# Gating, transposes and sums of h in steps of one K block, and a fourth branch's chunks moved between two passes, in a hybrid decoder layer on one core

## The chip, the cores and the metric

The kernel runs on one core of one Trainium2 chip. A core has a matrix engine (TensorE; PE in the rows, PEld for its weight loads), a vector engine (VectorE, DVE), a scalar engine (ScalarE, ACT), a general engine (GpSimd, POOL) and a sync engine (SyncE, SP) that here only issues DMAs. Each engine works through its own queue in the order in which the program was written. The metric is the device time of one execution in microseconds (us), lower is better; the median of three runs is compared.

## The reference

One layer, 512 tokens, width 2048, everything in float32. Four mixers run side by side on one normalised input; their outputs are normalised per branch and go through one output projection; then a SwiGLU FFN of width 5632 and a last normalisation.

```python
h = rmsnorm(x, norm_mix_g[l])
proj = h @ w_in[l]
pa, pb, pc, pd = jnp.split(proj, IN_SPLITS, axis=-1)
ya = merge_heads(mixer_dilated(*split_qkv_heads(pa), bias_a))    # branch A
yb = mixer_sgu(pb, ...)                                          # branch B
yc = merge_heads(mixer_moba(*split_qkv_heads(pc), bias_c))       # branch C
yd = mixer_rwkv7(pd, ...)                                        # branch D
ycat = rmsnorm(jnp.stack([ya, yb, yc, yd], axis=2), branch_norm_g[l]...)
x = x + ycat.reshape(B, S, D_MIX) @ w_out[l]
h = rmsnorm(x, norm_ffn_g[l])
x = x + (jax.nn.silu(h @ w_gate[l]) * (h @ w_up[l])) @ w_down[l]
return rmsnorm(x, norm_final_g)
```

## The kernel before

Each matrix product is made of three matmuls on operands that are split into a high and a low part: high by high, high by low, low by high. `split2` (L1041) makes the parts: ScalarE copies the source into the high part (L1043), VectorE subtracts it from the source for the low part (L1044). A weight chunk or block is loaded by SyncE, split by ScalarE and VectorE, and then used by TensorE in the program's order; `run` (L933) calls every generator in the list `side` once after each half block of matmuls. So the order of all work around the matmuls is set by where a generator yields.

**Output projection.** 32 chunks of 512 rows by 256 columns, in the order of the list `chunks`. The first pass has 8 column groups g of three chunks (branches D, B, C, numbered 3, 1, 2); `add_x2` adds its sums to the residual `x2`. Beside it the generator `attention(0, 0)` computes branch A, in 45 steps. The second pass has 8 chunks, branch A alone, one per g, and feeds the FFN: `on_last` (L1278) calls `make_x2` (add, gain, store of x), `split_a11`, `first_sums` of the group before, and the squares. `gemm` (L132) takes chunks from `next_chunk`, which issues the split of the chunk after it; the split's two tiles are taken from four (`wsp`), so they are free again when the matmuls of a chunk are done. After this pass `late_sums` runs in `side`: the last `first_sums`, eight sums of the second kind, eight splits.

**FFN up.** The products with `w_gate` and `w_up` are a Strassen-like scheme of seven products P1 to P7 on halves of tokens (th 0 and 1), of K and of gate and up. The 5632 columns are 11 groups `gi`; in each the seven products come in the order P1, P5, P6, P3, P7, P4, P2, each as four blocks (`strassen(k)`) of two K tiles, 12 matmuls of 128x128 by 512 columns to a block. `w_ahead(k)` sums the weights of block k+3 (`w_sum`: T for P5, P6, P4, in place for P7) and splits those of block k+2 (`w_split`, high part in one of 3 tiles, low in one of 4), and lets SyncE load up to block k+8, with at most 12 raw tiles of the 79 of the pool `p2`, which hold nearly all else too. `got_product` takes the results: c11 is kept after P1, c22 after P5, c12 after P6; P3 and P7 are added to c12 and c22. After P4, and after P2's add to c11, `gated` applies Silu (ScalarE, L1223) and the multiply (VectorE, L1224) to each of the two token tiles, one after the other, and appends `turn_h`, which waits four half blocks, then transposes 2 x 8 tiles on TensorE and calls `h_sums` (L1182) each time: the sums and splits that the down projection's own seven products need, each stored to DRAM (`ad`) by a DMA that ScalarE issues.

**FFN down.** `ds` lists 7 x 22 products (p, kk) in an order: P1 with P5, P6 with P3, then P7 and P4 with P2 strewn in after every second one. `d_ahead(i)` loads up to item i+4 and splits up to i+2 (T, high part `dh`, low part `dl`). Items 0 and 1 are begun under the last FFN blocks (`begin_down`); then `finish_all` runs out the `side` list, the pools `sums` (with `fp`) and `mid` (with `p2`) are closed, and the pool `dn` is opened on their memory. The last three items are done tile by tile at the end (`tail`), and after each of four token tiles `finish_tok` takes the mean square, scales and stores.

## Time and profile before

| what | value |
|---|---|
| runs before | 2351.2, 2355.08, 2352.35 us; median 2352.35 |
| the profiled execution | 2354.43 us, its span 2352.7 us, mean granted clock 0.985 |
| TensorE, PEld busy in the span | 2245.9 us (95%), 1793.7 us (76%) |
| VectorE, ScalarE busy | 1567.0 us (67%), 1013.7 us (43%) |
| high part 128x512, 128x1024 on ScalarE | 0.62, 1.06 us |
| low part 128x512, 128x1024 on VectorE | 0.69, 1.22 us |
| last store issued, end of span | 2348.68, 2352.7 us |

Times in the rows count from the start of the span. A matmul's record overlaps with the next one's, so stops of TensorE are best seen from start to start. A row of a timeline ends, in brackets, with the idle time before it on its engine and what ended that. A store or load is issued in a fraction of a microsecond and lands later. The two clock levels of TensorE are 1.2 and 2.4 GHz; the granted clock in the rows is the mean share of the higher one.

### The profile page before, as it was taken

What the parts mean: (1) busy time and instruction counts of PE and PEld (TensorE: products, weight loads), DVE (VectorE), ACT (ScalarE), POOL (GpSimd) and SP (SyncE); (2) the same over time, 40 slices, a digit from 0 to 9 for tenths busy, and PEclk for the clock granted to TensorE, in tenths of its full rate; (3) what the DMA queues carried; (4) which work ended last, traced back from release to release, by engine and by line L of the source; (5) the groups of instructions that cost most, each with busy time, mean ns of one, the idle gap of its engine ahead of it and who ended that gap; (6) DMA issues with size and microseconds to landing.
All of it is one profiled execution on the core that took longest, in us unless ns stands there. A gap on an engine that the chain in (4) does not pass through costs nothing.

```text
span 2352.7 us, 29300 instructions
## 1 busy us (share of the span) xinstructions
PE 2245.9 (95%) x11064; PEld 1793.7 (76%) x11064; DVE 1567.0 (67%) x2341; ACT 1013.7 (43%) x1556; POOL 2.3 (0%) x16
## 2 busy tenths in 40 slices
PE   8999999999999997899999999999999879999996
PEld 6788878877777785678777777877877768888785
DVE  6555456654444447877867877777787667777775
ACT  5522222244444435544444444444445344543334
POOL 0000000000000000000000000000000000000000
PEclk9999999999999999999999999999999989999998
DMA  5232323232233235343444455354355187547884
GB/s 185 84 95 73 101 76 92 61 99 82 71 99 108 90 109 178 118 164 121 166 161 152 149 169 180 114 189 166 117 170 192 52 289 250 175 130 241 284 299 177
DMA packets 164541, 342.78 MB, mean 146 GB/s; under 512 B 29296, under 2 KB 34928, under 8 KB 164400
## 3 DMA queue, kind: packets, MB, share of 16 engines
q1 hardware_dynamic: 134832, 290.25, 38.6%
q10 hardware_dynamic: 29568, 50.66, 6.0%
q8 instruction: 87, 1.43, 0.3%
q14 instruction: 54, 0.44, 0.1%
HBM read 302.79 MB, written 38.05 MB: 145 GB/s over the span
## 4 chain that ended last, share of the span: by engine, by line
PE 73%; DVE 13%; ACT 7%; issue 4%; DMA 1%; ACTq 1%; SPq 0%; DVEq 0%
PE prod L1266 8%; PE prod L1267 8%; PE prod L1265 8%; PE acc L144 7%; PE acc L146 7%; PE acc L145 7%; PE bk L1340 4%; PE bk L1341 4%; PE bk L1339 4%; DVE wl L1044 3%; PE acc L162 3%; PE acc L164 2%; PE acc L163 2%; ACT wh L1043 2%; DVE dl L1044 2%
## 5 line engine op out<-in xcount | busy, mean ns | idle before, releaser
L1044 DVE TENSOR_TENSOR wl<-wq,wh 128x512 fp32r<-128x512 f32 x352 | 227.2, 687 | 116.2 <-ACT wh L1043 115.2
L1266 PE MATMUL prod<-wl,h 128*128 128x512 f32 x704 | 282.1, 401 | 22.3 <-DVE wl L1044 22.2
L1265 PE MATMUL prod<-wh,h 128*128 128x512 f32 x704 | 281.5, 400 | 16.4 <-ACT wh L1043 16.4
L1267 PE MATMUL prod<-wh,l 128*128 128x512 f32 x704 | 279.3, 397 | 0.0
L1043 ACT ACTIVATE wh<-wq 128x512 fp32r<-128x512 f32 x352 | 201.4, 623 | 176.0 <-PE prod L1267 105.5
L1339 PE MATMUL bk<-dh,ah 128*128 128x512 f32 x608 | 238.7, 393 | 19.2 <-ACT dh L1043 19.2
L106 DVE TENSOR_TENSOR wlo<-wraw,whi 128x1024 fp32r<-128x1024 f32 x127 | 155.3, 1223 | 140.1 <-ACT whi L105 139.8
L1340 PE MATMUL bk<-dl,ah 128*128 128x512 f32 x608 | 240.0, 395 | 3.7 <-DVE dl L1044 3.7
L1341 PE MATMUL bk<-dh,al 128*128 128x512 f32 x608 | 237.9, 391 | 0.0
L105 ACT ACTIVATE whi<-wraw 128x1024 fp32r<-128x1024 f32 x127 | 134.0, 1055 | 210.7 <-PE acc L145 105.4
L144 PE MATMUL acc<-xhi,whi 128*128 128x512 f32 x512 | 209.3, 409 | 5.6 <-ACT whi L120 5.2
L1043 ACT ACTIVATE wh<-T 128x1024 fp32r<-128x1024 f32 x132 | 139.8, 1059 | 156.9 <-PE prod L1267 111.5
L146 PE MATMUL acc<-xhi,wlo 128*128 128x512 f32 x512 | 200.8, 392 | 1.1 <-DVE wlo L106 1.1
L145 PE MATMUL acc<-xlo,whi 128*128 128x512 f32 x512 | 200.6, 392 | 0.4 <-DVE xlo L235 0.3
L1044 DVE TENSOR_TENSOR wl<-T,wh 128x1024 fp32r<-128x1024 f32 x132 | 161.4, 1223 | 38.3 <-ACT wh L1043 37.7
L1266 PEld LDWEIGHTS prod<-wl,h 128*128 128x128 f32 x704 | 135.3, 192 | 58.9 <-DVE wl L1044 30.9
L1265 PEld LDWEIGHTS prod<-wh,h 128*128 128x128 f32 x704 | 135.1, 192 | 53.7 <-ACT wh L1043 25.5
L1267 PEld LDWEIGHTS prod<-wh,l 128*128 128x128 f32 x704 | 135.2, 192 | 27.7
L1339 PEld LDWEIGHTS bk<-dh,ah 128*128 128x128 f32 x608 | 115.0, 189 | 44.5 <-issue 17.4
L1265 PE MATMUL prod<-wh,hb 128*128 128x512 f32 x352 | 139.7, 397 | 6.7 <-DVE c L1234 6.7
L1043 ACT ACTIVATE dh<-T 128x1024 fp32r<-128x1024 f32 x66 | 70.0, 1061 | 174.1 <-DVE T L1418 57.2
L1340 PEld LDWEIGHTS bk<-dl,ah 128*128 128x128 f32 x608 | 115.0, 189 | 32.3 <-DVE dl L1044 9.2
(316 smaller groups left out, 4159.5 us busy)
## 6 DMA issues: line engine op xcount, KB each, us to landing
wq<-in_wgu_dram SPq DMA_DIRECT2D x440, 256.0 KB, 3.6
rw<-in_wdn_dram SPq DMA_DIRECT2D x134, 512.0 KB, 4.8
wraw<-in_wi_dram SPq DMA_DIRECT2D x63, 512.0 KB, 3.7
wraw<-in_wt_dram SPq DMA_DIRECT2D x32, 512.0 KB, 3.6
wraw<-in_wo_dram SPq DMA_DIRECT2D x32, 512.0 KB, 3.6
ar<-ad SPq DMA_DIRECT2D x44, 256.0 KB, 4.1
ad<-sh ACTq DMA_DIRECT2D x33, 256.0 KB, 3.9
ad<-sl ACTq DMA_DIRECT2D x33, 256.0 KB, 4.1
```

What stands on the lines that cost most here:

```text
L106: dv.tensor_sub(lo, r, hi.bitcast(F32))
L144: pe.matmul(acc[b], wh, xh, start=(c == 0 and k == 0), stop=False)
L145: pe.matmul(acc[b], wh, xl, start=False, stop=False)
L146: pe.matmul(acc[b], wl, xh, start=False, stop=(c == nchunk - 1 and k == 3))
L1043: ac.activation(hi, src, AF.Copy)
L1044: dv.tensor_sub(lo, src, hi.bitcast(F32))
L1265: pe.matmul(acc[t], ah[:, tt], hi[:, u], start=first, stop=False, skip_group_check=more)
L1266: pe.matmul(acc[t], ah[:, tt], lo[:, u], start=False, stop=False, skip_group_check=more)
L1267: pe.matmul(acc[t], al[:, tt], hi[:, u], start=False, stop=(j == 7), skip_group_check=more)
L1339: pe.matmul(o, ah[:, a], hi[:, cc], start=fresh, stop=False, skip_group_check=True)
L1340: pe.matmul(o, ah[:, a], lo[:, cc], start=False, stop=False, skip_group_check=True)
L1341: pe.matmul(o, al[:, a], hi[:, cc], start=False, stop=last, skip_group_check=True)
```

## The change

In `chunks` and the two loops, the branch C chunks of groups 5, 6 and 7 move from the first pass to the second, ahead of branch A's chunk of the same group. `gemm` gets a call `early`, made before the last block's `on_block`: it issues the split of a further chunk, or, when none is left, of the next FFN block. Five of the eight sums of the second kind (`last_sums`) move from `late_sums` into `on_last` of groups 6 and 7. `gated` and `h_sums` go; `turn_h` now does the gating, the transposes, the sums, splits and stores, each in a half-block step of its own. The pools `fp` and `dn` get `reuse_waits="tile"`: a tile then waits for the former users of its own memory, where by default a pool's first tiles wait until all pools whose memory it takes are free. In the down projection P2 is strewn in more densely and ends four items before the end; the first token half is finished there (`norm_tok`, `store_tok`), and the tail has three P4 items.

```diff
-        for br in (3, 1, 2):
+        for br in (3, 1, 2)[:3 - (g > 4)]:
             chunks.append(wo[g, br])
     for g in range(8):
-        chunks.append(wo[g, 0])
+        for br in (2, 0)[g < 5:]:
+            chunks.append(wo[g, br])
...
                 if c == nchunk - 1:
+                    if early and b:
+                        del hi, lo, wh, wl
+                        early()
                     on_block(b, acc[b])
...
-    fp = sums.enter_context(tc.tile_pool(name="fp", bufs=4))
+    fp = sums.enter_context(tc.tile_pool(name="fp", bufs=4, reuse_waits="tile"))
...
+    def last_sums(j):
+        h34, l34 = t2("h34", dt=F32R), t2("l34", dt=F32R)
+        a, s12 = xg.pop(j), s2.pop(j)
+        dv.tensor_sub(s12[:, hi_t], a[:, lo_t], a[:, hi_t])
+        split2(h34, s12, l34)
...
     def late_sums():
         first_sums(7)
         yield
-        for j in range(8):
...
+        for j in range(5, 8):
+            last_sums(j)
...
+    def turn_h(gi, th, h, us):
...
+        if th == 0:
+            yield
+            for t in range(2):
+                ac.activation(h[t], h[t], AF.Silu, scale=rn[t])
+        yield
+        for t in range(2):
+            dv.scalar_tensor_tensor(h[t], us[t], rn[t], h[t], op0=OP.mult, op1=OP.mult)
+        us.clear()
+        yield
+        yield
+        p = turned(0)
+        a = t2("hT")
+        ac.activation(a, p, AF.Copy)
+        if th:
+            yield
+            yield
+            yield
+            p = turned(1)
+            hi = high("P4", p)
+            yield
             s1 = held["S1"] = t2("hs")
-            parts("P4", ph)
-            dv.tensor_add(s1, ph, held["A21"])
+            dv.tensor_add(s1, p, a)
+            held["A21"] = a
+            yield
             put("P5", s1)
+            lo = low(p, hi)
+            yield
+            put("P4", lo.bitcast(F32), 1)
+            return
+        put("P1", a)
+        yield
+        s2, s3 = t2("hs"), t2("hs")
+        dv.tensor_sub(s3, a, held.pop("A21"))
+        yield
+        hi = high("P7", s3)
+        dv.tensor_sub(s2, held.pop("S1"), a)
+        yield
+        put("P6", s2)
+        lo = low(s3, hi)
+        yield
+        put("P7", lo.bitcast(F32), 1)
+        p = turned(1)
+        hi = high("P2", p)
+        yield
+        s4 = t2("hs")
+        dv.tensor_sub(s4, p, s2)
+        yield
+        put("P3", s4)
+        lo = low(p, hi)
+        yield
+        put("P2", lo.bitcast(F32), 1)
...
                 if g == 6:
-                    w_split(0)
-                    sw["add"] = sw["split"] = 1
-        run(gemm(1, lambda c, k: (yh[0, k], yl[0, k]), on_last))
...
+                    for j in range(3):
+                        last_sums(j)
+            elif g == 7:
+                for j in range(3, 5):
+                    last_sums(j)
+
+        def early(g=g):
+            if st["split"] < len(chunks):
+                issue_split()
+            else:
+                w_split(sw["split"])
+                sw["add"] = sw["split"] = sw["split"] + 1
+        brs = (2, 0)[g < 5:]
+        run(gemm(len(brs), lambda c, k: (yh[brs[c], k], yl[brs[c], k]), on_last, early))
...
-        if i % 2 and i > 2 or i == len(rest) - 4:
+        while n2 < NK and i >= 3 + n2 * 36 // (NK - 1):
             ds.append(("P2", n2))
             n2 += 1
...
-    dn = ctx.enter_context(tc.tile_pool(name="dn", bufs=1))
+    dn = ctx.enter_context(tc.tile_pool(name="dn", bufs=1, reuse_waits="tile"))
...
+        elif p == "P2" and i == ends["P2"]:
+            for t, c in each():
+                dv.tensor_add(cf[0, 0, t, c], V[t][c], cf[0, 0, t, c])
+                square(0, 0, t, c, cf[0, 0, t, c])
+            norm_tok(0, 0)
+            store_tok(0, 0, None)
+        elif p == "P4" and kk == NK - 1 - NT:
+            norm_tok(0, 1)
+            store_tok(0, 1, None)
...
+    for t in range(2):
+        for c in range(2):
+            for i in tail:
+                product(i, [(t, c)])
+            cf[1, 0, t, c] = dt("c", "c")
+            square(1, 0, t, c, U[t][c])
+        norm_tok(1, t)
+        if t == 0:
+            store_tok(1, t, U[t])
+    store_tok(1, 1, U[1])
```

## Rows read from the trace of the kernel before

**Rows 1.** Waits of TensorE: engine, line, what it waited for; total us, times, longest.
```profile
PE prod L1266 <- DVE wl L1044: 23.6, 27, 2.2
PE prod L1265 <- ACT wh L1043: 20.4, 23, 3.6
PE bk L1339 <- ACT dh L1043: 19.2, 3, 17.0
PE prod L1265 <- DVE c L1234: 6.7, 11, 2.4
```

**Rows 2.** Windows: stretch, length, busy us of the engines, granted clock, DMA.
```profile
870.44:923.93 53.49, 46.41 (x193) 34.89 (x191) 35.54 (x59) 29.81 (x50) 0.00 (x0) 1.00 0.53 168
923.93:1003.65 79.72, 64.94 (x248) 49.52 (x249) 69.98 (x114) 39.95 (x64) 0.00 (x0) 0.91 0.37 122
1003.65:1086.54 82.89, 79.49 (x352) 64.41 (x353) 64.68 (x94) 40.09 (x60) 0.00 (x0) 1.00 0.48 159
1003.65:1843.87 840.22, 804.59 (x3521) 650.97 (x3521) 647.92 (x931) 396.58 (x591) 0.00 (x0) 0.99 0.47 155
1866.72:1900.00 33.28, 13.63 (x43) 9.70 (x43) 14.11 (x17) 8.54 (x12) 0.00 (x0) 0.69 0.55 197
2321.10:2352.70 31.60, 13.38 (x50) 10.05 (x48) 14.60 (x28) 15.97 (x31) 0.00 (x0) 0.75 0.36 133
```

**Rows 3.** Timeline of TensorE from P1's end into P5 of group 1.
```profile
1037.88 0.39 PE L1266 MATMUL prod<-wl,a 128*128 128x512 f32 x1
1038.11 0.39 PE L1267 MATMUL prod<-wh,a 128*128 128x512 f32 x1
1038.93 0.50 PE L1265 MATMUL prod<-wh,h 128*128 128x512 f32 x1 [0.44 <-ACT wh L1043]
1040.19 0.50 PE L1266 MATMUL prod<-wl,h 128*128 128x512 f32 x1 [0.76 <-DVE wl L1044]
...
1043.98 0.49 PE L1265 MATMUL prod<-wh,h 128*128 128x512 f32 x1 [1.00 <-ACT wh L1043]
1045.24 0.50 PE L1266 MATMUL prod<-wl,h 128*128 128x512 f32 x1 [0.77 <-DVE wl L1044]
```

**Rows 4.** Timeline of VectorE over the same P1 and P5.
```profile
1028.31 0.75 DVE L1224 SCALAR_TENSOR_TENSOR c<-c,rn,c 128x512 f32<-128x512 f32 x1 [0.79 <-ACT c L1223]
...
1031.12 1.29 DVE L1044 TENSOR_TENSOR wl<-wq,wh 128x512 fp32r<-128x512 f32 x2
1032.33 1.29 DVE L1123 TENSOR_TENSOR T<-wq 128x512 f32<-128x512 f32 x2
...
1038.91 1.22 DVE L1044 TENSOR_TENSOR wl<-T,wh 128x1024 fp32r<-128x1024 f32 x1 [0.29 <-ACT wh L1043]
```

**Rows 5.** Timeline of ScalarE there.
```profile
1037.82 1.06 ACT L1043 ACTIVATE wh<-T 128x1024 fp32r<-128x1024 f32 x1 [1.13 <-DVE sl L1044]
```

**Rows 6.** Timeline of TensorE, first product of the down projection's loop.
```profile
1894.98 0.77 PE L1339 MATMUL bk<-dh,ah 128*128 128x512 f32 x1 [16.95 <-ACT dh L1043]
```

**Rows 7.** Waits of SyncE's DMA queue: total us, times, longest.
```profile
SPq L1114 <- DMA ad<-sh: 100.8, 30, 6.4
...
SPq L1389 <- DMA ad<-hs: 37.1, 1, 37.1
```

**Rows 8.** Timeline of SyncE, first loads of the pool dn.
```profile
1885.44 0.81 SPq L1389 DMA_DIRECT2D rw<-in_wdn_dram  x2
```

**Rows 9.** Timeline of VectorE, the first work on those loads.
```profile
1891.96 0.69 DVE L1044 TENSOR_TENSOR al<-ar,ah 128x512 fp32r<-128x512 f32 x1 [8.70 <-DMA rw<-in_wdn_dram]
```

**Rows 10.** Timeline of VectorE, low parts of two neighbouring chunks, second pass.
```profile
894.55 1.23 DVE L106 TENSOR_TENSOR wlo<-wraw,whi 128x1024 fp32r<-128x1024 f32 x1 [0.23 <-ACT whi L105]
...
902.00 1.23 DVE L106 TENSOR_TENSOR wlo<-wraw,whi 128x1024 fp32r<-128x1024 f32 x1 [0.23 <-ACT whi L105]
```

**Rows 11.** Timeline of ScalarE at the end.
```profile
2330.86 1.28 ACT L1474 ACT_TABLE_LOAD   x1
```

**Rows 12.** Timeline of VectorE, low part of the last P4 block.
```profile
2324.38 1.23 DVE L1044 TENSOR_TENSOR dl<-T,dh 128x1024 fp32r<-128x1024 f32 x1 [1.21 <-ACT dh L1043]
```

More of the change, by code (lines that the diff above doesn't have):

```diff
@@ L1004, in add_x2 @@
             dv.tensor_add(x2[g + 8 * b], acc, x2[g + 8 * b])
-        run(gemm(3, rhs_y, add_x2))
+        run(gemm(3 - (g > 4), rhs_y, add_x2))
     finish_all()
-    for br in (3, 1, 2):
+    for br in (3, 1):
         for f in range(4):
@@ L1165, in hybrid_kernel, with put, high, low @@
     part = {}
-    def turn_h(gi, th, h):
-        for _ in range(4):
-            yield
-        for b in range(2):
+    held = {}
+    def turn_h(gi, th, h, us):
+        def put(p, t, u=0):
+            nc.scalar.dma_start(ad[PI[p] + u, gi], t.rearrange("p (b t) -> p b t", b=2))
+        def high(p, src):
+            hi = t2("sh", dt=F32R)
+            ac.activation(hi, src, AF.Copy)
+            put(p, hi.bitcast(F32))
+            return hi
+        def low(src, hi):
+            lo = t2("sl", dt=F32R)
+            dv.tensor_sub(lo, src, hi.bitcast(F32))
+            return lo
+        def turned(b):
             p = px("ph")
@@ L1176, in turn_h @@
                                  h[t][:, (2 * b + fb) * 128:(2 * b + fb + 1) * 128], ident)
-            h_sums(gi, th, b, p)
+            return p
+        rn = [norm2.r[:, 2 * th + t:2 * th + t + 1] for t in range(2)]
+        if th == 0:
             yield
-    held = {}
-    def h_sums(gi, th, b, ph):
-        def put(p, t, u=0):
-            nc.scalar.dma_start(ad[PI[p] + u, gi], t.rearrange("p (b t) -> p b t", b=2))
-        def parts(p, src):
-            hi, lo = t2("sh", dt=F32R), t2("sl", dt=F32R)
-            split2(hi, src, lo)
-            put(p, hi.bitcast(F32))
-            put(p, lo.bitcast(F32), 1)
-        if (th, b) == (1, 0):
-            held["A21"] = t2("hT")
-            ac.activation(held["A21"], ph, AF.Copy)
-        elif (th, b) == (1, 1):
+            for t in range(2):
+                ac.activation(h[t], h[t], AF.Silu, scale=rn[t])
@@ L1235, in got_product @@
         elif p == "P4":
-            c = part["c21", t] = t2("c21")
-            gated(c, acc, part.pop(("c22", t)), 2 + t)
+            part["c21", t] = t2("c21")
+            ac.activation(part["c21", t], acc, AF.Silu, scale=norm2.r[:, 2 + t:3 + t])
             if t:
-                side.append(turn_h(gi, 1, [part.pop(("c21", 0)), part.pop(("c21", 1))]))
+                side.append(turn_h(gi, 1, *([part.pop((n, u)) for u in range(2)] for n in ("c21", "c22"))))
         else:
-            c = part["c11", t]
-            dv.tensor_add(c, acc, c)
-            gated(c, c, part.pop(("c12", t)), t)
+            dv.tensor_add(part["c11", t], acc, part["c11", t])
             if t:
-                side.append(turn_h(gi, 0, [part.pop(("c11", 0)), part.pop(("c11", 1))]))
+                side.append(turn_h(gi, 0, *([part.pop((n, u)) for u in range(2)] for n in ("c11", "c12"))))
     bank = {}
@@ L1475, in finish_tok, with store_tok @@
         dv.reciprocal(r[:, 3:4], r[:, 2:3])
+    def store_tok(th, t, bank):
+        r = rn4[th, t][:, 3:4]
         tok = slice((2 * th + t) * 128, (2 * th + t + 1) * 128)
-        for c in range(2):
-            o = cf.pop((th, 1, t, c))
-            ac.activation(o, o, AF.Copy, scale=r[:, 3:4])
-            nc.scalar.dma_start(out[tok, 1024 + c * 512:1536 + c * 512], o)
-        for c in range(2):
-            o = cf.pop((th, 0, t, c))
-            dv.scalar_tensor_tensor(o, bank[c] if bank else o, r[:, 3:4], gain[0][:, c * 512:(c + 1) * 512], op0=OP.mult, op1=OP.mult)
-            nc.sync.dma_start(out[tok, c * 512:c * 512 + 512], o)
+        for dh, c in ((1, 0), (0, 0), (0, 1), (1, 1)):
+            o = cf.pop((th, dh, t, c))
+            if dh == 0:
+                dv.scalar_tensor_tensor(o, bank[c] if bank else o, r, gain[0][:, c * 512:(c + 1) * 512], op0=OP.mult, op1=OP.mult)
+            elif c:
+                dv.tensor_scalar(o, o, r, None, op0=OP.mult)
+            else:
+                ac.activation(o, o, AF.Copy, scale=r)
+            col = dh * 1024 + c * 512
+            (nc.sync if dh + c < 2 else nc.scalar).dma_start(out[tok, col:col + 512], o)
     gain = []
@@ L1545, in hybrid_kernel @@
     d_ahead(len(ds) - NT)
-    for th, bank in ((0, V), (1, U)):
-        for t in range(2):
-            for c in range(2):
-                for i in tail:
-                    if (ds[i][0] == "P4") == bool(th):
-                        product(i, [(t, c)])
-                o = bank[t][c]
-                if th:
-                    cf[1, 0, t, c] = dt("c", "c")
-                    square(1, 0, t, c, o)
-                else:
-                    dv.tensor_add(cf[0, 0, t, c], o, cf[0, 0, t, c])
-                    square(0, 0, t, c, cf[0, 0, t, c])
-            finish_tok(th, t, bank[t] if th else None)
+    for t in range(2):
[8 more added lines that the diff above has]
+    store_tok(1, 1, U[1])
 def _constants():
```

39 lines of the change are left out of this document (9 added, 30 removed).

## The prediction

> **What bounds the kernel now.** I read the waits of TensorE first. Its longest sums are VectorE's low parts `wl` (23.6 us in 27 stops) and ScalarE's high parts `wh` (20.4 us in 23), both from `split2` in the FFN, and one stop of 17.0 us for `dh` [rows 1]. No row has TensorE waiting for a weight load. Then I cut the span into stages with the windows and asked in each what a dense TensorE would need [rows 2]. Two neighbouring matmuls start 0.23 us apart when nothing is late (1037.88, 1038.11) [rows 3], so a block of 12 takes 2.72 us (0.227 each), a chunk of 24 5.44 us. The second pass of the output projection (870.44 to 923.93) has 8 chunks, 43.5 us of matmuls, and takes 53.49; VectorE is busy for 35.54 of it. The first 20 blocks of the FFN (923.93 to 1003.65) take 79.72 us at a granted clock of 0.91 with VectorE busy 69.98, so VectorE is the bound there. After that ten groups take 840.22 us, 84.0 each, and VectorE is busy 647.92, 77%: on average it has room, so its stops must come from order. The down projection begins in a stretch of 33.28 us of which TensorE works 13.63.
>
> In a steady group the stop is always in one place, the first two blocks of P5 [rows 3]: idle 0.44, 0.76, 1.00 and 0.77 us. Counted by starts the first pair costs 0.82 + 1.26 less twice 0.23, 1.62 us for 1.20 of idle; the second pair, 1.77 of idle, on the same footing 2.19: 3.8 us in all. VectorE's rows say why [rows 4]: the gating of P2 goes add, Silu, multiply twice, and VectorE stands 0.79 us each time for ScalarE's Silu; then `h_sums` puts a chain of subtractions and splits, each waiting for the other engine, ahead of the P5 weights. ScalarE's `wh` for P5 waits 1.13 us for VectorE's `sl` [rows 5]. So the bound is two in-order queues that wait for each other in turn, and not the amount of work.
>
> **Gating and sums in steps.** Nothing is added in arithmetic: each Silu, multiply, add, split and store of a group is still there once. I walk VectorE's queue from the end of P2 (time 0). Two ops of 128x512 take 1.21 us (1031.12 to 1032.33), a multiply 0.75, an op of 128x1024 1.22 [rows 4]. The half-steps of 1.36 us fix the order: two `c11` adds 1.21, the low part of P4 0.6, `wl` of P1's third block 1.21, two multiplies 1.5 (their Silus ran in the half-step before, so no wait), T of P5's first block 1.21, `wl` of P1's fourth 1.21, T 1.21, `wl` of P5's first block 1.22: 9.4 us. TensorE gets there after four blocks and two sets of eight transposes, at about 11.9. The second P5 block adds s3, s2, T and `wl` (3.6): 13.0 against 14.6. The third adds a low part, T, `wl` and some 0.5 of waiting for the high part of P2: 16.5 against 17.4. The fourth adds s4, a low part, T and `wl`: 20.1 against 20.1. From P6 on a block costs VectorE 1.21 + 1.22 = 2.43 of 2.72, so the margin grows. ScalarE's queue is held by the stores, each behind its result (the store of s4 until about 17), and by the high parts, but stays ahead of VectorE in this walk. The margins are thin, so I leave 0.5 us of the stop per group. The stop of 0.6 us at P4 (6.7 us in 11 [rows 1]) comes from P4 accumulating onto P7's bank while VectorE reads it, and stays.
>
> What it is worth: the first steady group takes 82.89 us with the clock at 1.00; less 3.8 that is 79.1, with 0.5 left 79.6. The mean of ten is 84.0, because the lower clock that follows the stops stretches some (0.99 over the ten) [rows 2]. I take 84.0 - 79.6 = 4.4 plus 0.3 of pipeline restarts: **-47 us for ten groups**. Bounds: -25 if about half of the stops stay, -51 if all go.
>
> A consistent gap can have another cause. The row on the `wh` wait names VectorE's `sl` as what ended it, not a matmul that frees a tile [rows 5]. By the Trainium skill (Perfetto Trace Analysis, Optimization Strategy) the same gap repeated on the engine that should be full can mean that there is no room for the next tile; the change holds tiles longer, so by that rule this term would be 0 or worse. By the row the term stays as worked out; the rule is a rival below.
>
> **Last group into the down projection.** Here the gates, transposes and sums of the last group stand bare, and the pool `dn` waits for all of the pools whose memory it takes: SP's first `wdn` load waited 37.1 us for the landing of a store [rows 7] and went out at 1885.44 [rows 8]; the data ended a wait of 8.70 us on VectorE at 1891.96 [rows 9], and after al, T (1.22) and `dh` (1.06, from the table of durations) TensorE began at 1894.98, 16.95 us idle [rows 6]. With waits per tile the loads can go early, and what is late next is VectorE's and ScalarE's own chain. From P2's end (1866.72): both adds by 1869.5 (today they stand behind the splits of the first down blocks), Silus and multiplies by 1871.5, transposes behind the two down products at 1874.4, then copy, s3, split, s2, s4, split, with the stores between, to 1877.9; ah, al 1.5, T 1.2, `dh` 1.1: TensorE starts again at 1881.7. **-13 us.** Bounds: -5 if one of the first weight, T or ah tiles lies on memory of a late store (issued about 1878, load after it), -18 if ScalarE's chain is also shorter. The same argument for `fp` gives 0: its memory belonged to pools closed long before, and no row shows a wait for it.
>
> **Branch C chunks, early splits, moved sums.** Three chunks (16.3 us of matmuls) leave the first pass, where TensorE is dense, and go to block pairs 5 to 7 of the second. Their cover is not free: attention A has 45 side steps, and the first pass now gives 42, so its last three splits run bare; ScalarE and VectorE do them in about 3.3 us while TensorE uses the earlier ones: +1 us. In the second pass VectorE's chain is 7.45 us a chunk (894.55 to 902.00, `wlo` to `wlo`) [rows 10] against 5.44. The early split removes TensorE's wait on the split while there is a lead of one chunk, but puts the 2.3 us of `whi` and `wlo` in front of the second x2 add and its followers, so the chain is not shorter (I get some 8.8 us a chunk: whi 1.07, wlo 1.15, add, xg, a, sums, h, l, square, add, xg). The three extra chunks give this chain 16.3 us of TensorE to hide in; `last_sums` for 0 to 4 (some 1.7 us each: subtract 0.4, high 0.6, low 0.7) use 8.4 of them and disappear from the FFN's first blocks. In sum the same VectorE work starts 15 us earlier in time and waits a little more: I get the third P6 block of group 0 about 4 us sooner: **-4 us**. Bounds: -12 (VectorE as dense as today's 70 of 80 us [rows 2]), +4 (the 8.8 us chain sets everything).
>
> **Down order and tail.** P2 ends before the last four P4 blocks, so a token half is normalised and stored earlier. Its price is in VectorE's queue: the four adds (2.4), a reciprocal that waits for the root behind a table load of 1.28 us [rows 11], and three scalings (1.9) stand before T and the split of the last but one P4, and the second token before the last. A P4 block is a chain T, `dh`, `dl` of some 3.6 us, in which `dl` waits 1.21 for `dh` [rows 12]; T of the last but one starts about 7.2 us after P2's end, of the last 13.5, its low part is ready at 16.9. TensorE then has 27 matmuls and about 2.5 us of lower clock: last matmul at 26, square, root and scaling 4.1, last store to end 4.0 (from 2348.68 to 2352.7 today): 34.1 us. Today 31.60 from the same point, 48 matmuls before the end [rows 2]. **+2.5 us**; bounds -9 (all of the first half's work fits in VectorE's gaps) and +5. Elsewhere the down phase is dense, and a denser P2 there moves nothing.
>
> **The sum.** -47 - 13 - 4 + 2.5 = -61.5. The profiled execution took 2354.43 (span 2352.7 and 1.7 around it): 2292.9. It is 2.1 above the median of the runs shown, so I say **2291 us**. From no change a measurement tells about 0.2%, 4.7 us.
>
> **Rivals.**
> (a) As above: 2278 to 2306, chance 0.42.
> (b) The loads of `dn` still wait for a late store, -5 instead of -13: 2299. Tiles of the last group are a good part of that pool; against it: only a few tiles are needed at first. 0.10.
> (c) VectorE's margin of 0 to 0.9 us at the third and fourth P5 block is used up by waits for ScalarE, and half of the group term is lost: 2314, up to 2324. The thin walk speaks for it, the 77% of VectorE against. 0.20.
> (d) Better: the tail's work hides (-9) and the FFN's start gains 12: 2271 to 2278. 0.14.
> (e) The gap comes from too few tiles; the P5 stop stays, the other terms hold: 2291 + 47 = 2338. 0.07. It is what the rule of the Trainium skill named above would give.
> (f) Slower. Tiles held until their store has landed make the weight loads late; today such a load waits up to 6.4 us for a store [rows 7]. No row has an engine waiting for `wq`, so there is slack; beyond it each us costs one us a group, 11 in all, and at 5.6 us a group everything gained is gone. 0.07, of which 0.02 within 0.2%.
>
> Faster 0.93, same 0.02, slower 0.05. From (d) to (c) the range 2270 to 2324 leaves out the outer cases and edges, 2 in 10.
>
> **What would show it.** After: no stop over 0.3 us at P5's first blocks and groups of 79 to 80 us at a clock of 1.00; an idle stretch of about 7 us, not 17, before the first down product of the loop, ended by `dh` behind T and not by a load; P6's third block of group 0 near 968; two stops of 5 to 6 us at the last two P4 blocks. Wrong if SP's waits for stores grow to where `wh` or T waits for a load, or if P5 still waits for `wl`.

## The result and the profile after

After the change the kernel takes 2318.74 us (median of four runs, 2318.57 to 2319.38) against 2353.72 for the kernel before in the same job: a ratio of 0.9852, 95% interval 0.9835 to 0.9869, 35 us less. Predicted were 2291 us, with a range of 2270 to 2324: the side was right and the time lies in the range, but 35 us were gained where 61.5 were worked out. The profiled execution took 2319.38 us, its span is 2317.6.

The stages again, cut as in [rows 2], but for the fourth row here: it ends at the first product of the loop (1894.98 in the kernel before, where [rows 2] runs on to 1900.00). The columns are the stretch, its length, then busy time and instructions of each engine (PE, PEld, DVE, ACT, POOL), the granted clock, the DMA share and GB/s. The rows are: second pass of the output projection, here with three chunks more; first 20 FFN blocks; ten groups; from the first down product to the first one of the loop; the last 48 matmuls and what follows.

```profile
854.50:931.96 77.46, 63.94 (x266) 49.84 (x264) 47.36 (x77) 37.45 (x60) 0.00 (x0) 0.96 0.45 147
931.96:1003.90 71.94, 62.74 (x248) 48.47 (x249) 64.64 (x103) 36.12 (x58) 0.00 (x0) 0.93 0.39 125
1003.90:1812.48 808.58, 791.40 (x3521) 643.71 (x3521) 641.67 (x931) 399.72 (x592) 0.00 (x0) 1.00 0.49 161
1835.39:1857.22 21.83, 7.18 (x33) 5.28 (x33) 11.27 (x16) 5.74 (x8) 0.00 (x0) 0.76 0.66 233
2281.05:2317.60 36.55, 14.78 (x49) 10.14 (x47) 17.65 (x34) 14.17 (x28) 0.00 (x0) 0.72 0.31 115
```

Set against the kernel before, stage by stage, this is where the 35.1 us of span went (a stage runs from the start of its first matmul to that of the next stage's first):

| stage | before | after | difference | predicted |
|---|---|---|---|---|
| start to the first P4 block of group 0 | 1003.65 | 1003.90 | +0.25 | -4 |
| ten FFN groups | 840.22 | 808.58 | -31.64 | -47 |
| last group to the third down product | 51.11 | 44.74 | -6.37 | -13 |
| down loop | 426.12 | 423.83 | -2.29 | 0 |
| last 48 matmuls to the end | 31.60 | 36.55 | +4.95 | +2.5 |

The waits of TensorE that answer to [rows 1] (who waited for whom: us in all, times, the longest):

```profile
PE bk L1382 <- ACT dh L1047: 25.5, 3, 13.0
PE prod L1298 <- DVE wl L1048: 19.7, 25, 2.2
PE prod L1297 <- ACT wh L1047: 8.9, 2, 7.1
```

`wh` fell from 20.4 us to 8.9, of which 7.1 are one stop. `wl` still has 25 stops: two in each of the ten groups, and the start. `dh` is 25.5 instead of 19.2, in three stops.

**A steady group.** P5's first two blocks are dense now (0.13 and 0.02 us above 2.72 from start to start, where [rows 3] has idle times of 0.44 to 1.00). But the third block loses 1.16 us and the fourth 0.81, the same in all ten groups. Here is the third on TensorE (start, duration, line, operation, in brackets the idle time before it and what ended it):

```profile
1044.35 0.51 PE L1297 MATMUL prod<-wh,h 128*128 128x512 f32 x1
1045.61 0.50 PE L1298 MATMUL prod<-wl,h 128*128 128x512 f32 x1 [0.75 <-DVE wl L1048]
```

VectorE's queue around it:

```profile
1039.93 1.23 DVE L1048 TENSOR_TENSOR wl<-T,wh 128x1024 fp32r<-128x1024 f32 x1 [0.36 <-ACT wh L1047]
1041.07 0.68 DVE L1190 TENSOR_TENSOR sl<-hs,sh 128x512 fp32r<-128x512 f32 x1
1041.67 1.29 DVE L1131 TENSOR_TENSOR T<-wq 128x512 f32<-128x512 f32 x2
1044.33 1.22 DVE L1048 TENSOR_TENSOR wl<-T,wh 128x1024 fp32r<-128x1024 f32 x1 [1.37 <-ACT wh L1047]
1045.47 0.68 DVE L1246 TENSOR_TENSOR hs<-ph,hs 128x512 f32<-128x512 f32 x1
...
1047.88 1.22 DVE L1048 TENSOR_TENSOR wl<-T,wh 128x1024 fp32r<-128x1024 f32 x1
```

And ScalarE's, its DMA issues (ACTq) among them:

```profile
1039.80 1.06 ACT L1257 ACTIVATE c<-prod 128x512 f32<-128x512 f32 x2
1041.79 0.35 ACTq L1180 DMA_DIRECT2D ad<-sl  x1
1042.24 0.60 ACT L1184 ACTIVATE sh<-ph 128x512 fp32r<-128x512 f32 x1 [1.37 <-DMA wq<-in_wgu_dram]
1042.87 0.33 ACTq L1180 DMA_DIRECT2D ad<-sh  x1
1043.24 1.06 ACT L1047 ACTIVATE wh<-T 128x1024 fp32r<-128x1024 f32 x1 [0.40 <-ACT sh L1184]
1046.19 0.33 ACTq L1180 DMA_DIRECT2D ad<-hs  x1
1046.56 1.06 ACT L1047 ACTIVATE wh<-T 128x1024 fp32r<-128x1024 f32 x1 [2.27 <-DVE hs L1246]
```

VectorE stands 1.37 us with T long made (the third block's T was done at 1039.57; the T at 1041.67 is the fourth's), because ScalarE's `wh` for the third block starts only at 1043.24. ScalarE was free from 1040.87. But the next thing in its queue is the store of P7's low part, and that waits for VectorE's `sl`, done at 1041.75; then come P2's high part and its store. The row puts ScalarE's 1.37 us down to a load; the store issued right ahead, at 1041.79, is what it stood behind. The fourth block has no such wait: from 1044.33 on VectorE works without a pause, and its `wl` at 1047.88 is late by what was lost at the third. (The `wh` of that block, behind the store of s4 at 1046.19, was ready at 1047.62, before VectorE came to it.) A store in ScalarE's queue makes ScalarE wait for VectorE, and VectorE for ScalarE.

**Second pass and the FFN's start.** From low part to low part VectorE's chain is now 8.93 us (886.16 to 895.09), 7.45 in [rows 10]:

```profile
886.16 1.23 DVE L107 TENSOR_TENSOR wlo<-wraw,whi 128x1024 fp32r<-128x1024 f32 x1 [1.73 <-ACT whi L106]
...
889.08 0.42 DVE L1048 TENSOR_TENSOR a<-xg,a 128x256 fp32r<-128x256 f32 x1 [1.09 <-ACT a L1047]
...
891.00 0.69 DVE L1048 TENSOR_TENSOR l<-s,h 128x512 fp32r<-128x512 f32 x1 [0.70 <-ACT h L1047]
...
895.09 1.23 DVE L107 TENSOR_TENSOR wlo<-wraw,whi 128x1024 fp32r<-128x1024 f32 x1 [1.74 <-ACT whi L106]
```

Of 8.93 us 3.5 are three waits for copies of ScalarE. Then TensorE stands 7.15 us before the first FFN block, which starts at 931.96 (923.93 before):

```profile
931.96 0.79 PE L1297 MATMUL prod<-wh,a 128*128 128x512 f32 x1 [7.15 <-ACT wh L1047]
```

**Last group.** TensorE is idle 12.98 us, not 16.95 [rows 6]. The third and fourth of the last group's ten stores, SP's first loads of the down loop (a row joins neighbours; the second starts at 1846.71), and TensorE's restart:

```profile
1840.16 0.33 ACTq L1180 DMA_DIRECT2D ad<-sl  x1
...
1844.47 0.33 ACTq L1180 DMA_DIRECT2D ad<-hT  x1
```

```profile
1842.23 4.81 SPq L1432 DMA_DIRECT2D rw<-in_wdn_dram  x2
1847.91 0.33 SPq L1448 DMA_DIRECT2D ar<-ad  x1
```

```profile
1857.22 0.79 PE L1382 MATMUL bk<-dh,ah 128*128 128x512 f32 x1 [12.98 <-ACT dh L1047]
```

**Tail.** Two stops before the last two weight blocks, and VectorE's queue that makes the first of them, with the first half's adds, reciprocal and scalings ahead of T. P2 ended at 2281.05, but the adds stand behind the low part of a block further ahead:

```profile
2293.42 0.79 PE L1382 MATMUL bk<-dh,ah 128*128 128x512 f32 x1 [8.79 <-ACT dh L1047]
...
2299.60 0.79 PE L1382 MATMUL bk<-dh,ah 128*128 128x512 f32 x1 [3.69 <-ACT dh L1047]
```

```profile
2282.60 1.23 DVE L1048 TENSOR_TENSOR dl<-T,dh 128x1024 fp32r<-128x1024 f32 x1 [1.21 <-ACT dh L1047]
2283.74 2.47 DVE L1590 TENSOR_TENSOR c<-bk,c 128x512 f32<-128x512 f32 x4
...
2289.08 0.16 DVE L1519 RECIPROCAL s<-s 128x1 f32<-128x1 f32 x1 [2.60 <-ACT s L1518]
2289.28 1.41 DVE L1528 SCALAR_TENSOR_TENSOR c<-c,s,gain 128x512 f32<-128x512 f32 x2
...
2291.00 1.22 DVE L1472 TENSOR_TENSOR T<-rw,T 128x1024 f32<-128x1024 f32 x1
```

### The profile page after: what moved, and what is told of

The parts are those of the page before. It is cut to its first block, busy times and chain, and to the rows that moved or that the text cites. A ratio compares the mean times of both kernels' runs of the same rounds, so it can differ in the third digit from the quotient of the medians.

```text
span 2317.6 us, 29310 instructions
## 1 busy us (share of the span) xinstructions
PE 2231.3 (96%) x11064; PEld 1787.2 (77%) x11064; DVE 1562.3 (67%) x2345; ACT 1014.6 (44%) x1552; POOL 2.3 (0%) x16
## 4 chain that ended last, share of the span: by engine, by line
PE 82%; DVE 9%; ACT 4%; DMA 2%; issue 2%; ACTq 0%; SPq 0%; DVEq 0%
PE prod L1298 10%; PE prod L1299 10%; PE prod L1297 10%; PE acc L145 7%; PE acc L147 7%; PE acc L146 7%; PE bk L1383 5%; PE bk L1384 5%; PE bk L1382 5%; PE acc L166 3%; PE acc L168 3%; PE acc L167 3%; DVE wl L1048 2%; DMA wq<-in_wgu_dram 1%; ACT wh L1047 1%
## 5 line engine op out<-in xcount | busy, mean ns | idle before, releaser
L1298 PE MATMUL prod<-wl,h 128*128 128x512 f32 x704 | 276.8, 393 | 17.4 <-DVE wl L1048 17.4
L1297 PE MATMUL prod<-wh,h 128*128 128x512 f32 x704 | 276.4, 393 | 0.0
L1299 PE MATMUL prod<-wh,l 128*128 128x512 f32 x704 | 274.2, 390 | 0.0
L1382 PE MATMUL bk<-dh,ah 128*128 128x512 f32 x608 | 239.7, 394 | 25.5 <-ACT dh L1047 25.5
```

Source lines behind the costliest of these rows:

```text
L1297: pe.matmul(acc[t], ah[:, tt], hi[:, u], start=first, stop=False, skip_group_check=more)
L1298: pe.matmul(acc[t], ah[:, tt], lo[:, u], start=False, stop=False, skip_group_check=more)
L1299: pe.matmul(acc[t], al[:, tt], hi[:, u], start=False, stop=(j == 7), skip_group_check=more)
L1382: pe.matmul(o, ah[:, a], hi[:, cc], start=fresh, stop=False, skip_group_check=True)
```

## The experiments

Eleven kernels ran, each in four or five timed runs beside the kernel before, which took 2352.8 to 2353.6 us in these jobs; so a difference of 1 us between jobs says nothing. Times below are set against the changed kernel's 2318.74.

**Stores behind the splits.** Every store of h goes on a list, which is issued after the splits of the next block; the loop that runs out `side` at the end issues it too.

```diff
         def put(p, t, u=0):
-            nc.scalar.dma_start(ad[PI[p] + u, gi], t.rearrange("p (b t) -> p b t", b=2))
+            o, x = ad[PI[p] + u, gi], t.rearrange("p (b t) -> p b t", b=2)
+            stores.append(lambda: nc.scalar.dma_start(o, x))
...
         w_ahead(k)
+        put_all()
```

> The changed kernel, with every store of h put on a list and issued right after the splits of the next block, so that ScalarE copies the high part of a block before it issues the stores; the amount of work is the same. Theory A (ScalarE's queue: at P5's third and fourth block the high part stands behind a store that waits for VectorE's low part or sum): the stops of 1.16 and 0.81 us per group go, 10 groups, -15 to -19 us against the changed kernel, about 2301 us, groups of 79.0 us. Theory B (VectorE simply has too much to do there): the stops stay, 2319. Theory C (too few tiles, and the stores now hold them longer): the stops stay or grow, 2319 or more.

Measured: 2298.06 us (2297.57 to 2298.39), 20.7 less; ratio to before 0.9765 (0.9751 to 0.978). A group takes 78.8 us, and P5 has no stop left. ScalarE at the same place, and then the ten groups as a window:

```profile
1039.79 0.60 ACT L1191 ACTIVATE sh<-ph 128x512 fp32r<-128x512 f32 x1
1040.27 1.07 ACT L1047 ACTIVATE wh<-T 128x1024 fp32r<-128x1024 f32 x1
1040.89 0.33 ACTq L1187 DMA_DIRECT2D ad<-sl  x1
```

```profile
1004.01:1792.49 788.48, 784.07 (x3520) 645.27 (x3521) 639.16 (x931) 394.33 (x592) 0.00 (x0) 1.00 0.51 165
```

`wh` of the third block starts at 1040.27 instead of 1043.24, the store behind it. VectorE does the same work (639.16 us, 641.67 in the changed kernel), so B falls; tiles are held longer than in the changed kernel, so C falls. It is a little more than A gave, 20.1 us of it in the ten groups.

**The same edit on the kernel before.** Its `put`, `strassen` and the loop at the end get the same lines, nothing else.

> The kernel before, with nothing changed but that the stores of h are put on a list and issued right after the splits of the next block. Theory A (what stops P5 in the kernel before, too, is ScalarE's queue behind stores alone): the stops at P5's first two blocks go, groups of 79 to 80 us instead of 84.0, 2305 to 2315. Theory B (the gates and the chain of sums and splits in two lumps are the greater part, and the steps of the change are needed to take them apart): 0.5 to 1.5 us of the group, 82.5 to 83.5, 2337 to 2347. Theory C: no difference, 2353.

Measured: 2321.72 us (2321.6 to 2323.72), ratio 0.9869 (0.9856 to 0.9883). Between A and B, nearer to A: the groups take 81.1 us.

```profile
1003.96:1814.84 810.88, 791.09 (x3521) 645.19 (x3521) 645.66 (x931) 395.59 (x591) 0.00 (x0) 1.00 0.47 161
```

```profile
1118.73 0.69 DVE L1044 TENSOR_TENSOR sl<-hs,sh 128x512 fp32r<-128x512 f32 x1 [0.70 <-ACT sh L1043]
...
1123.03 0.69 DVE L1044 TENSOR_TENSOR sl<-ph,sh 128x512 fp32r<-128x512 f32 x1 [0.67 <-ACT sh L1043]
```

Moving the stores alone takes 29.3 us from the ten groups (840.22 to 810.88), the whole rewrite of the gating 31.6, both together 51.7. What is left without the steps is 2.2 us a group. Of it 1.9 are two stops at P5's first two blocks (0.4 and 1.4 from start to start), behind VectorE's two waits for a high part made in the same step. Did the two edits remove the same stop, both together would be worth some 31 us; were they wholly separate, 60.9. At 51.7 they take for the most part different pieces, and neither alone takes all.

**Without the early splits.**

```diff
                 if g == 6:
+                    w_split(0)
+                    sw["add"] = sw["split"] = 1
                     for j in range(3):
                         last_sums(j)
...
-        run(gemm(len(brs), lambda c, k: (yh[brs[c], k], yl[brs[c], k]), on_last, early))
+        run(gemm(len(brs), lambda c, k: (yh[brs[c], k], yl[brs[c], k]), on_last))
```

> The changed kernel without the early splits in the second pass of the output projection; the first FFN block is split in column group 6, as in the kernel before. Theory A (the early split puts a wait for the high part of 1.74 us into VectorE's chain and makes it 8.93 us a column group instead of 7.45): the chain goes back to 7.4 to 7.5 us from low part to low part, the FFN starts 5 to 8 us sooner than at 931.96, and the first P4 block of group 0 comes 3 to 5 us sooner than at 1003.90: about 2315 us. Theory B (the work of VectorE up to the third P6 block is fixed, and any time won in the second pass is given back in the FFN's first blocks): the FFN starts sooner but that P4 block stays within 1 us of 1003.90, 2319 us.

Measured: 2323.04 us (2322.46 to 2324.84), 4.3 more: neither theory. The chain did go back to 7.44 us (880.77 to 888.21), but the FFN started at 934.32 and the first P4 block of group 0 at 1006.92. VectorE's rows show what stands there:

```profile
921.17 0.41 DVE L1074 TENSOR_TENSOR s<-xg 128x256 f32<-128x256 f32 x1
...
925.78 0.69 DVE L1048 TENSOR_TENSOR l<-s,h 128x512 fp32r<-128x512 f32 x1 [0.76 <-ACT h L1047]
926.72 1.22 DVE L107 TENSOR_TENSOR wlo<-wraw,whi 128x1024 fp32r<-128x1024 f32 x1 [0.26 <-ACT whi L106]
```

The three `last_sums` of column group 6 (921.17 to 926.5) stand ahead of the split of the last chunk. The early split costs 1.5 us a column group and pays by going ahead of them. A kernel with neither the early splits nor the moved sums was not run.

**The moved sums put back.** No `last_sums` in `on_last`, `late_sums` does all eight.

> The changed kernel with the five sums of the second kind put back behind the second pass (all eight in late_sums); the early splits and the moved chunks stay. Run no_early showed that without the early splits the three sums of column group 6 stand in front of the split of the last chunk. Theory A (those sums in front of the first FFN block's split cause the stop of 7.15 us at 924.42): the stop falls under 2 us and the FFN starts at 925 to 927 instead of 931.96. What that is worth at the first P4 block of group 0 (1003.90): theory B, nothing, since VectorE has the same work to do before it, only later: within 1 us, 2319; theory C, the sums hide better where the change put them, since in the FFN's first blocks VectorE has no room: 2 to 5 us later, 2321 to 2324; theory D, most of the 7 us are kept: 2313 to 2315.

Measured: 2319.12 us (2318.17 to 2320.29), no difference. The FFN starts at 924.72, 7.2 us sooner, A; and the first P4 block comes at 1003.50, 0.4 sooner, B. What was won ahead of the FFN was given back in its first blocks.

**Another order in the second pass** (on the kernel *together*, below). The early split only issues ScalarE's copy; its low part waits in the list `lows`, which `first_sums` issues (`flush`) after its first two sums.

```diff
         dv.tensor_sub(s12[:, hi_t], s12[:, lo_t], a[:, lo_t])
+        if lows is not None:
+            flush()
...
             make_x2(g + 8 * b, acc)
             if b:
-                split_a11(g)
                 if g:
                     first_sums(g - 1)
+                else:
+                    flush()
+                split_a11(g)
...
-                if g == 6:
-                    for j in range(3):
+                if g in (5, 6):
+                    for j in range(2 * g - 10, 2 * g - 8):
                         last_sums(j)
             elif g == 7:
-                for j in range(3, 5):
-                    last_sums(j)
+                last_sums(4)
```

> The kernel of together, with another order in the second pass of the output projection: after the last block of a column group ScalarE first copies the high part of the next chunk, VectorE does the x2 add and the first two sums before that chunk's low part, and the low part of a11 comes after those of the sums; of the moved sums two come in each of groups 5 and 6 and one in 7. The work is the same. Theory A (VectorE is not full there, 3.5 us a group are waits for ScalarE's copies in its queue): the second pass becomes nearly dense, its stops of 8.8 us in all and the stop of 7.15 us before the FFN fall to under 6 together, and the first P4 block of group 0 comes 8 to 15 us sooner than at 1004.0: 2268 to 2275. Theory B (run sums_back: whatever is won ahead of the FFN is given back in its first blocks, where VectorE has too much to do): the FFN starts 8 to 12 us sooner but that P4 block within 3 us: 2280 to 2284.

Measured: 2267.95 us (2267.55 to 2268.31), 15.3 less than *together*; ratio to before 0.9639 (0.9626 to 0.9652). Second pass and first 20 blocks:

```profile
854.26:915.68 61.42, 60.20 (x266) 49.26 (x264) 46.77 (x77) 36.69 (x60) 0.00 (x0) 1.00 0.49 162
915.68:985.73 70.05, 60.91 (x250) 47.57 (x249) 64.54 (x103) 36.11 (x58) 0.00 (x0) 0.95 0.44 148
```

Eleven chunks at 5.44 us are 59.8; the pass takes 61.42 with VectorE's work nearly unchanged (46.77 us, 47.34 in *together*). The P4 block comes 18.3 us sooner than in *together* (1004.00 to 985.73), of which the last group gives back 1.4 (a stop of 10.95 us instead of 9.48) and the down loop 1.5. A, by a little more than it gave; B does not hold here: the FFN's first 20 blocks did not grow (70.05 us, 71.93 in *together*). The new order and the new places of the moved sums were not run apart.

The last group's longer stop has another cause than in the changed kernel. The first down load goes out at 1806.30, where its eighth DMA before, a store issued at 1794.99, would have let it go at about 1797 (see *paired_last* below). It waits for VectorE:

```profile
SPq L1487 <- DVE hs L1267: 32.0, 1, 32.0
```

That subtraction of the last group ends at 1806.23. A load into memory that it still uses would wait so, much as in rival (b), but no run shows that this is the reason.

**Waits of the pool `dn` as before.**

```diff
-    dn = ctx.enter_context(tc.tile_pool(name="dn", bufs=1, reuse_waits="tile"))
+    dn = ctx.enter_context(tc.tile_pool(name="dn", bufs=1))
```

> The changed kernel with the pool dn waiting, as before, until all the memory that it takes is free. Theory A (with waits per tile the first loads wait only for the DMA eight before each): now the first load waits for the landing of the last store of h, and goes out at 1851 to 1853 instead of 1842.23, all three loads behind it come together, and the down products restart 3 to 6 us later: 2322 to 2325. Theory B (the waits per tile change nothing, the last group's chain of sums and splits is what is late): 2318 to 2320.

Measured: 2323.11 us (2322.67 to 2323.37), 4.4 more. SP's loads:

```profile
1851.81 0.80 SPq L1432 DMA_DIRECT2D rw<-in_wdn_dram  x2
1852.66 0.42 SPq L1448 DMA_DIRECT2D ar<-ad  x1
```

All three go out together, behind the last store, and the restart is at 1861.53 instead of 1857.22. A.

**Paired stores in the last group.** In the last group the parts of P7, and of P2, lie in one tile each and leave in one store; the group has two steps less.

```diff
+        def pair(p, src):
+            hl = wp.tile([128, 2, 512], F32R, name="hl", tag="wraw", bufs=3)
+            split2(hl[:, 0], src, hl[:, 1])
+            return p, hl
+        def put_pair(p, hl):
+            o = ad[PI[p]:PI[p] + 2, gi].rearrange("u p b t -> p u (b t)")
+            nc.scalar.dma_start(o, hl.bitcast(F32))
```

> The changed kernel, where in the last group the high and low part for P7, and those for P2, lie in one tile each and go out as one store, with two steps less: eight stores stand between the last FFN block and the first loads of the down loop instead of ten. Theory A (a load waits for the DMA that is eight before it in the program's order, whatever memory it writes): the first weight load goes out before 1838 instead of at 1842.23, the second by 1841, the load of ar by 1843, the stop of 12.98 us falls to 7 to 9 us: 2314 us. Theory B (what is late is the last group's own chain of copies, sums and splits on ScalarE and VectorE, the loads come in time): the loads go out sooner, the stop shrinks by less than 1.5 us, 2317 to 2319. Theory C (the loads wait for the memory of late tiles): the loads go out when they did, 2319.

Measured: 2317.3 us (2315.99 to 2318.17), 1.4 less. Loads:

```profile
1835.95 5.32 SPq L1455 DMA_DIRECT2D rw<-in_wdn_dram  x2
1842.83 0.33 SPq L1471 DMA_DIRECT2D ar<-ad  x1
```

With two stores less the three loads went out at 1835.95, 1840.94 and 1842.83, behind earlier stores than before, and the stop fell from 12.98 to 8.95. This is A's mechanism, and the times of the stores bear it out. With ten stores ahead of the loads, the DMA eight before each load is the third, fourth and fifth store: they are issued at 1840.16, 1844.47 and 1845.86, and the loads go out 2.07, 2.24 and 2.05 us later. With eight stores it is the first three, issued at 1833.89, 1838.87 and 1840.66, and the loads follow 2.06, 2.07 and 2.17 us later. But only 1.4 us came through: the next loads of the loop wait in the same way, and its third and fourth products take 2.3 us longer again. What is left of the stop is the chain on VectorE and ScalarE, which now ends last.

**Two down products ahead** (on *second_order*; the third and fourth P1 product are loaded, split and put between the last group's transposes).

> The kernel of second_order, with two more down products (P1, the third and fourth) loaded and split ahead of the down loop and put between the transposes of the last group; only P7's parts still share one store. Theory A (the stop of 9.5 us there is the last group's own chain on VectorE and ScalarE, and 5.4 us of matmuls fit beside it): 3 to 5 us less than second_order. Theory B (the splits of the two products take VectorE's time from that chain, 1.2 us each and the low part of ar, and the loads are later still): within 1.5 us.

Measured: 2267.31 us (2266.46 to 2268.32), 0.6 less than *second_order*, within the spread. B: the longest stop is 6.44 us instead of 10.95, but the loop's first product starts at 1817.83, where second_order, with two products fewer done, had 1816.27, and products behind it stop for loads.

**The first half's end behind the last splits.**

```diff
         elif p == "P2" and i == ends["P2"]:
-            for t, c in each():
-                dv.tensor_add(cf[0, 0, t, c], V[t][c], cf[0, 0, t, c])
...
     d_ahead(len(ds) - NT)
+    for t, c in each():
+        dv.tensor_add(cf[0, 0, t, c], V[t][c], cf[0, 0, t, c])
+        square(0, 0, t, c, cf[0, 0, t, c])
+    for t in range(2):
+        norm_tok(0, t)
+        store_tok(0, t, None)
```

> The changed kernel with the adds, squares, norm and scaling of the first token half moved behind the splits of the last weight block, so that they stand beside the tail's matmuls. Theory A (these pieces in VectorE's queue make the weights of the last two P4 blocks late, stops of 8.79 and 3.69 us): both stops fall under 1 us, and as VectorE's 7 us of them fit beside 8.2 us of tail matmuls the end comes 8 to 11 us sooner, about 2309 us. Theory B (the weights of the last P4 blocks are late anyway, since their sum, high and low part take 3.6 us one after the other against 2.72 of matmuls): a stop of 3 us or more stays and the first half's work pushes the last stores out, 2315 to 2319.

Measured: 2316.15 us (2315.01 to 2316.56), 2.6 less. The stops shrank to 1.55 and 1.57 us, so the pieces in VectorE's queue did cause them, A; but the time is B's. Two stops of the chain T, `dh`, `dl` remain, and after the last matmul (2298.84) ScalarE's squares stood behind stores that waited for VectorE's scalings, the last store 10.3 us later.

**T one item ahead, all output stores by SyncE** (on *tail_later*).

```diff
         elif p == "P4":
-            src = Td.pop(kk)
-            dv.tensor_sub(src, rw_.pop(i), src)
+            src = d_sum(i)
+            if i + 1 < len(ds) and ds[i + 1][0] == "P4":
+                Td[ds[i + 1][1]] = d_sum(i + 1)
...
-            elif c:
+            elif c and not (th and t):
...
-            (nc.sync if dh + c < 2 else nc.scalar).dma_start(out[tok, col:col + 512], o)
+            nc.sync.dma_start(out[tok, col:col + 512], o)
```

> Run tail_later with three more edits: where two P4 items stand side by side, the sum T of the second is made before the low part of the first; all stores of the output go out by SyncE, so that ScalarE's squares don't stand behind a store that waits for VectorE; both second-half columns of the last token tile are scaled by ScalarE. Theory A (the two stops of 1.55 us come from sum, high and low part one after the other, and after the last matmul the squares stand 1 to 5 us behind stores): no stop over 0.8 us before the tail, and about 8 us instead of 14.1 from the last matmul to the end: 8 to 10 us less than tail_later, 2306 to 2308. Theory B (the scalings of the first half are simply too much beside 8 us of matmuls): 2312 or more.

Measured: 2306.37 us (2305.7 to 2306.67), 12.4 less than the changed kernel, 9.8 less than tail_later. No stop over 0.8 us before the tail. From the start of the last matmul (2291.55) to the end it is 13.4 us (14.5 in *tail_later*), not 8: the first half's scalings are still there, beside a TensorE that is done. The time was A's, its second step only in small part. The three edits were not run apart.

**Together**: stores behind the splits, paired stores, and this tail.

> Stores behind the splits, stores paired in the last group, and the tail of tail_ahead in one kernel. If the three causes are separate, the differences add: -20.7 and -1.4 from the runs before, -11 to -13 expected of the tail: 2284 to 2287. If the stores behind the splits also move the last group's stores against its loads, less of the second remains, up to 2290.

Measured: 2283.27 us (2282.72 to 2284.09), 35.5 less than the changed kernel; the three differences add to 34.5. The causes are separate.

## Why the prediction was right or wrong, point by point

**Gating and sums in steps, -47 predicted, -31.6 measured.** The reading of the kernel before was right: two in-order queues that wait for each other, not work and not tiles. It missed one thing. The `wh` of [rows 5] does not need `sl`, and the T it reads was made by 1033.62 [rows 4]; what stands ahead of it in ScalarE's queue is the store of `sl`:

```profile
1037.45 0.33 ACTq L1185 DMA_DIRECT2D ad<-sl  x1
```

Run before_stores shows that such stores alone held 29.3 us of the ten groups. Right too that P5's first two blocks become dense and that the clock is 1.00 in the ten groups. The step that failed is the walk past the second P5 block: "ScalarE's queue is held by the stores, each behind its result ..., and by the high parts, but stays ahead of VectorE in this walk". It doesn't. I allowed 0.5 us for ScalarE at the third block; `wh` of that block made VectorE wait 1.37, and the low part was ready 18.5 us after P2's end (1045.55 less 1027.04), not 16.5. Of these 2.0 us 0.9 are that wait. The other 1.1 were lost before it: 0.7 in the first block, since my walk left out an add of VectorE's (below), and 0.4 in the second, with a wait of 0.36 for its `wh`. With TensorE there at 17.3 neither part alone would have made more than a stop of about 0.1 us.

```profile
1027.35 0.68 DVE L1222 TENSOR_TENSOR hs<-ph,hT 128x512 f32<-128x512 f32 x1
```

Rival (c) named the place and the cause, with half the term lost; a third was. Run stores_behind shows the cause: with the stores moved both waits are gone, VectorE has no pause left there, and the groups are 78.8 us, under the 79.6 of the forecast. The 0.3 us of pipeline restarts in the term stand on no row. The rule of the Trainium skill behind rival (e), Perfetto Trace Analysis, section Optimization Strategy, that a repeated gap can mean no room for the next tile, did not apply: the stop went in a kernel that holds its tiles longer.

**Last group, -13 predicted, -6.4 measured.** Rival (b), loads that still wait for a late store, is what came, with nearly its price of -5; but not for the reason I gave it. The step that failed is "With waits per tile the loads can go early". The waits per tile are worth 4.3 us (dn_all), and then a load waits for the DMA eight before it, whatever memory it writes. The predicted restart is 15.0 us after P2's end, the measured one 21.8. Paired_last brought it to 17.8, so 4.0 us are the loads; the other 2.8 are VectorE's and ScalarE's chain, which ends 13.8 us after P2's end (1849.14) where I had 11.2. The transposes came when I said (7.8 us after P2's end, 7.7 in the walk); it is the copy, sums and splits behind them that take 5.9 us and not 3.5.

**Chunks, early splits, moved sums, -4 predicted, +0.25 measured.** The three bare steps of attention A cost 2.1 us by the start of the second pass's second block, not 1. The chain of "some 8.8 us a chunk" was right, 8.93. The step that failed is "The three extra chunks give this chain 16.3 us of TensorE to hide in". The sums did leave the FFN's first 20 blocks (71.94 us, 79.72 before [rows 2]), but they did not hide: they stand ahead of the first FFN weights, where TensorE is idle 7.15 us. VectorE got no denser, busy 112.0 of 149.4 us from the second pass to the first P4 block (105.5 of 133.2 before [rows 2]). P6's third block came at 976.10, not near 968 but 3.6 us later than before (972.55); that the stage ends at +0.25 comes from two stops behind that place, 1.2 us at that block and 2.0 of P4's wait for `c`, which went. Both runs that undo a part gain nothing, and the move of the chunks was not undone; second_order, where VectorE works while ScalarE copies, gains 18.3 us at that place, more than the bound of -12, which took today's 70 of 80 us for dense.

**Down order and tail, +2.5 predicted, +4.95 measured**, just inside the bound of +5. Mechanism and place were right, two stops at the last two P4 blocks; they are 8.79 and 3.69 us, not 5 to 6 each. The step that failed is the start of the walk: it counts the four adds from P2's end (2281.05), but they begin 2.7 us later (2283.74), behind the low part of a block ahead. So T of the last but one comes 9.95 us after P2's end, not 7.2, and T of the last 16.1, not 13.5. From the adds on the walk held: 6.2 us between the two, 6.3 in the forecast. The sentence "a denser P2 there moves nothing" missed 2.3 us of the down loop: two stops among its late blocks went, 1.3 and 0.9 us from start to start (2229.66 and 2157.13 in the kernel before).

**The sum, and rivals (d) and (f).** Of the 26.4 us missed, 15.4 are the groups, 6.6 the last group, 4.3 the chunks and 2.4 the tail; the loop gave 2.3 back. That the time lies between the two of rival (c), 2314 and 2324, is in part luck: (c) has all of the loss in the groups. Nothing spoke for (d) in the changed kernel. (f) did not happen: in the ten groups SP's loads wait up to 5.1 us for a store to land (6.4 before [rows 7]), and neither TensorE nor VectorE has a wait that a load ends.

## What to carry to other kernels

In these traces a DMA issue is an instruction in an engine's queue: where it waits for another engine, as ScalarE's at 1041.79 does, all that stands behind it waits too. When a walk of two queues gives margins under 1 us, walk both in program order with every store in its place. Issue stores behind the next piece that the other engine needs; a list and the place where it is issued did that here, and on the kernel before they were worth nearly as much as the rewrite (31 us and 35). And when a stage is bound by a queue's waits, not by its work, ask first which independent instructions could stand between a copy and its reader: the reorder of the second pass, with the moved sums spread anew, was worth 15 us, moving work into it nothing. The best version, *second_order*, takes 2267.95 us, with prestart no faster by more than the runs spread.

## What the runs showed of the hardware

A wait for several things is put down in the rows to one of them: ScalarE's 1.37 us at 1042.24 carry the name of a weight load, and vanish when a store is moved. The loads of SP and the stores of ScalarE, though on two queues, are tied: in the changed kernel and in paired_last each of the first three down loads goes out 2.05 to 2.24 us after the issue of the DMA eight before it. Taking two stores out of the last group moved a load of other data 6.3 us forward (1842.23 to 1835.95). It is not the only tie: in second_order the first load waited for VectorE. Why it is the eighth before, and whether every wait of SP in the loop is of this kind, no run shows.
